# Strassen FFN-out in passes of 8, 8 and 6 units, with all seven products doubled in its all-Strassen output pairs

## The chip, the core and the metric

The kernel runs on one core of a Trainium2 chip. Its time is the device time of one execution in microseconds (us), given as the median of several runs. A profile is the record of one further execution: its span runs from the first to the last instruction, and the execution's own time lies a little above the span. Five engines work side by side, each with its own in-order instruction stream: TensorE (PE, matrix products, with its weight loads listed as PEld), VectorE (DVE), ScalarE (ACT), GpSimd (POOL) and SyncE (SP). SP and POOL also issue the transfers between DRAM and the on-chip memory.

## What is computed

One layer of a decoder on 512 tokens of width 2048, in float32. Cut to what matters here:

```python
h = rmsnorm(x) ; proj = h @ w_in                    # 2048 -> 11264 columns
y_a, y_b = gated spatial mixing, stick-breaking attention
merged = sigmoid(g_a) * (y_a @ w_up_a) + sigmoid(g_b) * (y_b @ w_up_b)
x = x + merged @ w_o
hid = rmsnorm(x) @ w_ffn_in                         # 2048 -> 2 * 5632
x = x + (silu(hid[:5632]) * hid[5632:]) @ w_ffn_out # 5632 -> 2048
x = x + sigmoid(rmsnorm(x) @ w_ple_gate) * (p @ w_ple)
```

The change lies in the last two products, the FFN-out product (5632 to 2048) and the gate product (2048 to 2048), and in how operands for FFN-in and for these two are prepared.

## The kernel before

Activations lie transposed: 128 partitions of features by 512 tokens. A *unit* is a piece of 256 features of the contraction: 2048 features are 8 units (`KU`), the hidden layer's 5632 are 22. An *output pair* is 256 output features. Each operand is held as a high and a low part, and each product is taken as high times high, high times low and low times high (`mm3`, lines 272 to 282: three matrix products).

A unit is multiplied in one of two ways. Plain (P): four weight blocks of 128x128 against 512 tokens, 12 products of 512 columns. Strassen (S): seven products of sums of blocks, each against 256 tokens, 21 products of 256 columns; the seven are put together afterwards by `mix` on DVE and ACT. In a *doubled* Strassen product the high and low halves lie side by side, so high weights take both in one product of 512 columns and low weights one of 256: 14 products per unit for all seven (line 692), each product in a bank of its own, put together by `mix_doubled` (lines 726 to 770) in more and smaller DVE steps. `Pair.__init__` sets `doubled` to 0 as soon as one unit of the pair is plain, so only all-S pairs are doubled. Before the change FFN-in is doubled 7, the input projection 5, FFN-out and gate not at all. A pair with both kinds adds its plain banks at the end in `rest` (line 796).

Weights come by `Weights`: a transfer of raw blocks by SP, for S one more adding transfer by POOL, then splits on ACT (line 343) and DVE (340) and two sums on DVE (359). One such object serves one unit, or two neighbours of the same kind when the first has an even number (`doubles`). Four landing buffers and three slots hold them.

Operands come as `Form`s. A late S form first loads its raw unit (1024 columns of the arena `wholes`, `fetch`), splits it for plain use (`plain_first`, lines 270, 271), and later loads it once more (`fetch_second`) to build the three or four sums (line 509) that Strassen use needs. `PLAIN_UNTIL` says for how many output pairs a unit is used plain: in each FFN-out pass four units become S at pair 1, the others at pair 2. `all_first` (used for the input projection) builds everything from one load. Forms live in the arena `parts`, which holds eight S forms and 1024 columns more. After every one to three products `tick` runs (line 197): it may fetch one of the next three forms (`AHEAD`), build the first of them if its places are free, or else fetch a second load. Loads, weights and stores all go through SP's queue.

FFN-out contracts 22 units in passes of 8, 7 and 7 (`PASSES`). In a pass each of the eight output pairs j takes all units of the pass; passes 2 and 3 load the partial sum of pair j, add to it (`onto`, lines 801 and 805) and store it. In pass 3 the sum is also scaled (line 1225), the residual added (1439), the result x2 stored (1440) and squared for the next norm (957, 961). The next pass's forms join the queue `builds` at the last pair (j = 7), and the gate's eight forms, made of x2[0..7], do so at the last pair of pass 3. The gate is `SSSSSPPP`, with pair 0 all plain; its pair 0 needs all of x2.

Of the kernel before, what the change touches and what calls it, by code (L numbers as in the profile page):

```python
# [19 lines left out]
P = 128  # L20
# [3 lines left out]
KU = D // (2 * P)  # L24
HID = 5632
KH = HID // P
# [3 lines left out]
EPS = 1e-6  # L30

OUT = "SSSSPPPP"
PASSES = 8, 7, 7
PLAIN_UNTIL = 1, 1, 1, 1, 2, 2, 2, 2
GATE = "SSSSSPPP"
PLACE = 7 * 256

AHEAD, WAIT = 3, 2
# [28 lines left out]
def hybrid_layer(  # L67
# [131 lines left out]
    def tick():  # L199

        clock[0] += 1
        last, units = traced()[-1], dict(newest)
        urgent = [f for f in seconds if f.used]
        for f in list(builds)[: 0 if urgent else AHEAD]:
            if not f.there and f.ready() and fits([(wholes, 1024, "old")]):
                f.fetch()
                break
        if builds and builds[0].ready() and builds[0].arrived() and fits(builds[0].sizes):
            builds.popleft().step()
        elif seconds and fits([(wholes, 5 * 256, "old")]):  # L210
# [300 lines left out]
    def twice(x):  # L511
        return x.unsqueeze(1).to_broadcast([P, 2, 256])

    def plain_first(form, raw, gain=None):
# [36 lines left out]
    def all_first(form, raw):  # L551


        b, s, v = cut(raw.f()), take(768, "old"), take(256, "old")
        t, x = cut(s.f()), form.operand()
        split_into(x[:, 0:4, 0], x[:, 0:4, 1], b)
        tt(t[:, 2], b[:, 3], b[:, 2])
        tt(v.f(), b[:, 3], b[:, 1])
        tt(t[:, 0], t[:, 2], b[:, 1])
        tt(t[:, 1], t[:, 0], b[:, 0], ALU.add)  # L560
        give(raw)
        form.at_plain = True
        yield
        yield
        split_into(x[:, 4:7, 0], x[:, 4:7, 1], t)
        give(s)
        yield
        while not form.used:
            yield
        split_into(x[:, 3, 0], x[:, 3, 1], v.f())  # L570
        give(v)

    def late_form(src, ready=always, gain=None, far=False):

# [14 lines left out]
    def strassen_form(src, ready=always, gain=None, raw=PLACE):  # L589

# [216 lines left out]
    def pair(forms, last=False, plain=None, parts_done=None, at=0, home=lambda: None,  # L807
             doubled=0):

        plain = plain or (0,) * len(forms)
        kinds = "".join("P" if n else f.kind for f, n in zip(forms, plain))
        p = Pair(kinds, home, doubled)
        for k, n in doubles(kinds, at):
            slot, ws = next_weights()
            fs = forms[k : k + n]
            p.add(kinds[k], ws, [f.plain() if plain[k] else f.get() for f in fs])
            for f, left in zip(fs, plain[k : k + n]):
                if left == 1:  # L820
                    f.use_plain()
                if last:
                    f.free()
            slots.append(slot)
            if parts_done and k + n == kinds.find("P"):
                last_parts(p, forms[k + n :], parts_done)
                break
        return p

    def plain_left(n, j, until=PLAIN_UNTIL):  # L830

        return tuple(max(0, u - j) for u in until[:n])

    def kinds_of(forms_kinds, j, until=PLAIN_UNTIL):
        return "".join("P" if left else k
                       for k, left in zip(forms_kinds, plain_left(len(forms_kinds), j, until)))

    def last_parts(p, forms, done):

# [435 lines left out]
    def plan_rest():  # L1275
        for j in range(KU):
            for b in "ba":
                plan((w_up_a if b == "a" else w_up_b)[j], "PPPP")
        for j in range(KU):
            plan(w_o[j], OUT)  # L1280
        for j in range(3, KU):
            planned.append((w_ple[j].rearrange("p (b c) -> p b c", b=4), 1, "P"))
        for m in range(KH):
            plan(w_ffn_in[m], ("S" if m else "P") * KU)
        at = 0
        for n in PASSES:
            for j in range(KU):
                plan(w_ffn_out[j], kinds_of("S" * n, j), at)
            at += n
        for j in range(KU):  # L1290
            plan(w_gate[j], GATE if j else "P" * KU)

    def y_form(c, i):
        return plain_form((lambda: y_a[i]) if c == "a" else lambda: load(y_spill[i]),
# [68 lines left out]
             for j in range(KU)}  # L1363
    there = set()

    def spilled_form(kind, n, j, gain=None):
        return (late_form if kind == "S" else plain_form)(
            lambda size=1024: load(spill[n, j], size), lambda: (n, j) in there, gain, far=True)
# [19 lines left out]
    for j in range(5, 8):  # L1388
# [7 lines left out]
    hs = [spilled_form("S", "hid", u) for u in range(KH // 2)]  # L1396
# [9 lines left out]

    for m in range(KH):
        if m == KH - 1:
            builds.extend(hs[: PASSES[0]])
        o = pair(fs, last=m == KH - 1, plain=(0 if m else 1,) * KU, doubled=7).out()  # L1410
# [7 lines left out]
    gs = [spilled_form(k, "x2", j, (g_ple, j)) for j, k in enumerate(GATE)]  # L1418
    norm3 = Norm()
    at = 0  # L1420
    for c, n in enumerate(PASSES):
        units, first = hs[at : at + n], at
        at += n
        for j in range(KU):
            if j == KU - 1:
                builds.extend(hs[at : at + PASSES[c + 1]] if c + 1 < len(PASSES) else gs)
            before = load(spill["sum", j]) if c else None
            x1 = load(spill["x1", j]) if c == len(PASSES) - 1 else None
            pr = pair(units, last=j == KU - 1, plain=plain_left(n, j), at=first)
            if before is None:  # L1430
                nc.sync.dma_start(out=spill["sum", j], in_=pr.out())
                continue
# [14 lines left out]
    for j in range(KU):  # L1447
# [18 lines left out]
            nc.sync.dma_start(out=outT[j][:, a:b], in_=s)  # L1466

        if j == KU - 1:
            pair(gs, parts_done=finish)
# [92 lines left out]
```

## Time and profile before

| | |
|---|---|
| runs before | 2722.21 us median of 3 (2721.26 to 2723.8) |
| profiled execution | 2724.13 us, span 2722.2 us |
| mean granted TensorE clock | 0.994 |
| PE busy | 2668.2 us, 98% of the span |
| DVE busy | 2204.5 us, 81% |
| DMA | 557.74 MB, mean 205 GB/s |

Where the stages begin, by the first product of each in the trace: w_up at 825.1 us, w_o at 1000.8, FFN-in at 1182.1, FFN-out at 2054.9 (pass 2 at 2220.4, pass 3 at 2363.8), gate at 2524.3, end at 2722.2. A view of windows gives for each stretch its length, then busy time and count of instructions for PE, PEld, DVE, ACT and POOL, the granted clock (PEclk, 1.00 is full) and the DMA share with its rate. A view of waits lists what an engine waited for and how long. A busy PE is not a PE at full speed, so the length of a stretch is set against the work in it as well.

### The profile page before, as it was taken

The numbers are of one execution on the slowest core, as the hardware profiler recorded it, in microseconds if no ns is written. First come the engines' busy times: TensorE is split into PE (matmuls) and PEld (weight loads), VectorE is DVE, ScalarE is ACT, GpSimd is POOL, SyncE is SP. The second block draws the span as 40 slices with busy tenths as digits, with TensorE's granted clock in tenths as the row PEclk, the third lists the DMA queues.
The fourth block names the chain that finished last, engine by engine and source line by source line (L and its number), as shares of the span: only waits on it lengthen the run. The fifth ranks groups of instructions, "written<-read, shape, count | busy, mean of one in ns | idle before, by whom it ended". The sixth has DMA issues, their size and how long they took to land.

```text
span 2722.2 us, 44416 instructions
## 1 busy us (share of the span) xinstructions
PE 2668.2 (98%) x16334; PEld 2374.5 (87%) x16334; DVE 2204.5 (81%) x3685; ACT 1405.6 (52%) x2174; POOL 477.3 (18%) x566
## 2 busy tenths in 40 slices
PE   8999999999999999999999999999999999989899
PEld 7888888888998889978888888888888999989698
DVE  8687878788887566679989898989889778789776
ACT  7656565655554343385444444444445444444643
POOL 0232323232210000011111111111111102111110
PEclk9999999999999999999999999999999999999899
DMA  7676777777775466688888888787878879889884
GB/s 227 155 189 167 189 167 190 167 200 180 178 189 193 131 181 200 172 268 209 205 229 201 207 195 215 195 209 195 206 193 263 245 223 283 252 238 277 253 234 124
DMA packets 305883, 557.74 MB, mean 205 GB/s; under 512 B 26752, under 2 KB 155648, under 8 KB 305664
## 3 DMA queue, kind: packets, MB, share of 16 engines
q1 hardware_dynamic: 242496, 447.52, 51.1%
q0 software_dynamic: 63168, 107.37, 24.7%
q8 instruction: 128, 2.10, 0.3%
q14 instruction: 91, 0.75, 0.1%
HBM read 507.61 MB, written 47.19 MB: 204 GB/s over the span
## 4 chain that ended last, share of the span: by engine, by line
PE 86%; DVE 6%; DMA 3%; ACT 2%; issue 2%; POOL 1%; SPq 0%; DVEq 0%; ACTq 0%; POOLq 0%
PE ps L692 40%; PE ps L281 13%; PE ps L282 13%; PE ps L280 13%; PE small L692 4%; DVE wlo L340 2%; DVE parts L271 1%; DVE out L751 1%; DMA wholes<-hid 1%; DMA wholes<-x 1%; PE small L1158 1%; ACT whi L343 1%; PE small L1033 1%; DVE wholes L509 1%; PE small L1108 1%
## 5 line engine op out<-in xcount | busy, mean ns | idle before, releaser
L343 ACT ACTIVATE whi<-wholes 128x1280 fp32r<-128x1280 f32 (+3 forms) x960 | 876.1, 927 | 805.6 <-DVE wholes L359 273.7
L692 PE MATMUL ps<-parts,whi 128*128 128x512 f32 x3384 | 1135.5, 398 | 3.3 <-ACT out L789 2.6
L340 DVE TENSOR_TENSOR wlo<-wholes,whi 128x1280 fp32r<-128x1280 f32 (+3 forms) x960 | 984.3, 1059 | 86.5 <-ACT whi L343 86.0
L281 PE MATMUL ps<-parts,whi 128*128 128x256 f32 (+1 forms) x2799 | 881.2, 315 | 11.1 <-DVE parts L271 10.8
L280 PE MATMUL ps<-parts,whi 128*128 128x256 f32 (+1 forms) x2782 | 869.5, 315 | 21.3 <-ACT parts L270 15.7
L282 PE MATMUL ps<-parts,wlo 128*128 128x256 f32 (+1 forms) x2799 | 878.6, 315 | 0.6 <-DVE wlo L340 0.6
L692 PEld LDWEIGHTS ps<-parts,wlo 128*128 128x128 f32 x3384 | 635.8, 188 | 142.0 <-issue 1.0
L692 PE MATMUL ps<-parts,wlo 128*128 128x256 f32 x3384 | 671.2, 279 | 0.0
L281 PEld LDWEIGHTS ps<-parts,whi 128*128 128x128 f32 x2799 | 536.5, 192 | 51.7 <-DVE parts L271 15.1
L280 PEld LDWEIGHTS ps<-parts,whi 128*128 128x128 f32 x2782 | 531.3, 192 | 57.2 <-ACT parts L270 18.5
L282 PEld LDWEIGHTS ps<-parts,wlo 128*128 128x128 f32 x2799 | 535.6, 192 | 33.1 <-DVE wlo L340 2.5
L692 PEld LDWEIGHTS ps<-parts,whi 128*128 128x128 f32 x3384 | 546.7, 189 | 9.8 <-ACT out L789 3.0
L359 DVE TENSOR_TENSOR wholes<-wholes 128x256 f32<-128x256 f32 (+1 forms) x840 | 348.2, 415 | 24.2 <-issue 3.5
L347 POOL DMA_DIRECT2D wholes<-w_ffn_in x172 | 149.7, 870 | 698.9 <-DVE wholes L359 261.5
L751 DVE TENSOR_TENSOR out<-out,ps 128x256 f32<-128x256 f32 x388 | 160.2, 415 | 125.1 <-ACT out L748 124.6
L347 POOL DMA_DIRECT2D wholes<-w_in x132 | 118.4, 898 | 489.3 <-DMA wholes<-w_in 112.6
L271 DVE TENSOR_TENSOR parts<-wholes,parts 128x1024 fp32r<-128x1024 f32 (+4 forms) x126 | 132.3, 1058 | 25.2 <-ACT parts L270 25.0
L347 POOL DMA_DIRECT2D wholes<-w_ffn_out x79 | 74.1, 939 | 403.3 <-DMA wholes<-w_ffn_out 152.6
L270 ACT ACTIVATE parts<-wholes 128x1024 fp32r<-128x1024 f32 (+4 forms) x126 | 113.7, 920 | 51.0 <-DVE wholes L509 35.9
L692 PE MATMUL small<-parts,whi 128*128 128x512 f32 x344 | 136.2, 397 | 0.0
L718 DVE TENSOR_TENSOR out<-out 128x256 f32<-128x256 f32 x144 | 61.0, 423 | 84.0 <-ACT out L715 81.5
L1400 ACT ACTIVATE out<-out 128x512 f32<-128x512 f32 x44 | 27.9, 633 | 161.1 <-DVE out L1399 161.1
(122 smaller groups left out, 1697.4 us busy)
## 6 DMA issues: line engine op xcount, KB each, us to landing
wholes<-w_ffn_in SPq DMA_DIRECT2D x172, 384.0 KB, 5.6
wholes<-w_in SPq DMA_DIRECT2D x132, 384.0 KB, 5.0
wholes<-w_ffn_in SPq DMA_DIRECT2D x172, 256.0 KB, 4.8
wholes<-w_ffn_in POOLq DMA_DIRECT2D x172, 256.0 KB, 5.4
wholes<-w_in SPq DMA_DIRECT2D x132, 256.0 KB, 4.1
wholes<-w_in POOLq DMA_DIRECT2D x132, 256.0 KB, 4.9
wholes<-w_ffn_out SPq DMA_DIRECT2D x65, 384.0 KB, 5.3
wholes<-x SPq DMA_DIRECT2D x45, 512.0 KB, 5.5
```

What stands on the lines that cost most here:

```text
L270: return (nc.scalar.activation(hi, src, AF.Copy), nc.vector.tensor_tensor(out=lo, in0=src, in1=hi.bitcast(F32), op=ALU.subtract))
L271: nc.vector.tensor_tensor(out=lo, in0=src, in1=hi.bitcast(F32), op=ALU.subtract))
L280: nc.tensor.matmul(ps, sh, mh, start=start, stop=False)
L281: nc.tensor.matmul(ps, sh, ml, start=False, stop=False)
L282: return nc.tensor.matmul(ps, sl, mh, start=False, stop=stop)
L340: in_turn(nc.vector.tensor_tensor(out=self.lo[:, blocks], in0=r, in1=h.bitcast(F32), op=ALU.subtract))
L343: in_turn(nc.scalar.activation(h, r, AF.Copy))
L347: nc.gpsimd.dma_start(out=raw[:, 3:5], in_=self.src[:, 1:3], accum_op=ALU.add)
L359: in_turn(nc.vector.tensor_tensor(out=o, in0=x, in1=y, op=ALU.add))
L692: m = nc.tensor.matmul(out, l, r, start=first and k == 0, stop=last and k == 1)
L718: in_turn(nc.vector.tensor_tensor(out=out, in0=x, in1=y, op=op))
L751: in_turn(nc.vector.tensor_tensor(out=out, in0=x, in1=y, op=op))
```

## The change

- The passes of FFN-out are 8, 8 and 6 units; in the last pass units 4 and 5 are plain throughout, and its first four units turn S at pair 2.
- All-S pairs of FFN-out are doubled in all seven products.
- The gate's forms join `builds` at the start of the last pass. In the gate, units 2, 3 and 4 stay plain in pair 1 as well.
- FFN-in's forms are built by `all_first` from one load; `all_first` itself loses one step of waiting between its two splits, in the input projection too.
- `tick` fetches a form only if places in `parts` for it and for those ahead of it are free along with the raw buffer, or if three raw buffers fit (`fits` adds one more of 1024 columns to what it is asked).
- `plain_left` and `kinds_of` give way to `now`; `pair` is told j and until when each unit is plain.

```diff
-PASSES = 8, 7, 7
-PLAIN_UNTIL = 1, 1, 1, 1, 2, 2, 2, 2
+PASSES = "SSSSSSSS", "SSSSSSSS", "SSSSPP"
+PLAIN_UNTIL = (1, 1, 1, 1, 2, 2, 2, 2), (1, 1, 1, 1, 2, 2, 2, 2), (2, 2, 2, 2, 1, 1)
 GATE = "SSSSSPPP"
+GATE_UNTIL = 1, 1, 2, 2, 2, 1, 1, 1
...
         urgent = [f for f in seconds if f.used]
+        sizes = []
         for f in list(builds)[: 0 if urgent else AHEAD]:
-            if not f.there and f.ready() and fits([(wholes, 1024, "old")]):
+            sizes += [s for s in f.sizes if s[0] is parts]
+            raw = [(wholes, 1024, "old")]
+            if not f.there and f.ready() and (fits(sizes + raw) or fits(raw * 3)):
                 f.fetch()
                 break
...
         give(raw)
         form.at_plain = True
         yield
-        yield
         split_into(x[:, 4:7, 0], x[:, 4:7, 1], t)
...
-    def late_form(src, ready=always, gain=None, far=False):
+    def late_form(src, ready=always, gain=None, far=False, twice=True):
...
-            yield from plain_first(form, w, gain)
+            yield from plain_first(form, w, gain) if twice else all_first(form, w)
             return form.operand()
 
-        return Form("S", steps, [(parts, 2 * PLACE, "place")] + [(wholes, 1024, "low")], ready,
-                    src, far)
+        return Form("S", steps, [(parts, 2 * PLACE, "place")]
+                    + [(wholes, 1024, "low")] * (1 if twice else 2), ready, src, far)
...
-            p.add(kinds[k], ws, [f.plain() if plain[k] else f.get() for f in fs])
-            for f, left in zip(fs, plain[k : k + n]):
-                if left == 1:
+            p.add(kinds[k], ws, [f.plain() if j < until[k] else f.get() for f in fs])
+            for f, m in zip(fs, until[k : k + n]):
+                if j == m - 1:
                     f.use_plain()
...
+    def now(kinds, until, j):
+
+        return "".join("P" if j < n else k for k, n in zip(kinds, until))
...
-    fs = [spilled_form("S", "x1", j, (g_ffn, j)) for j in range(KU)]
+    fs = [spilled_form("S", "x1", j, (g_ffn, j), twice=False) for j in range(KU)]
...
-    for c, n in enumerate(PASSES):
-        units, first = hs[at : at + n], at
-        at += n
+    for c, units in enumerate(hs):
+        first, at = at, at + len(units)
+        if c == len(hs) - 1:
+            builds.extend(gs)
         for j in range(KU):
-            if j == KU - 1:
-                builds.extend(hs[at : at + PASSES[c + 1]] if c + 1 < len(PASSES) else gs)
+            if j == KU - 1 and c < len(hs) - 1:
+                builds.extend(hs[c + 1])
...
-            pr = pair(units, last=j == KU - 1, plain=plain_left(n, j), at=first)
+            pr = pair(units, last=j == KU - 1, j=j, until=PLAIN_UNTIL[c], at=first,
+                      doubled=7)
...
-            o = pair(gs, plain=(0 if j else 1,) * KU).out()
+            o = pair(gs, j=j, until=GATE_UNTIL).out()
```

More of the change, by code (lines that the diff above doesn't have):

```diff
@@ L512, in twice, with plain_first @@
         return x.unsqueeze(1).to_broadcast([P, 2, 256])
-    def plain_first(form, raw, gain=None):
+    def plain_first(form, raw, gain):
         x = form.operand()
@@ L805, in onto, with pair @@
                     nc.vector.tensor_tensor(out=s, in0=s, in1=ps, op=ALU.add)
[L807 to L813, printed above, removed]
+    def pair(forms, last=False, j=0, until=None, parts_done=None, at=0,
+             home=lambda: None, doubled=0):
+        until = until or (0,) * len(forms)
+        kinds = now("".join(f.kind for f in forms), until, j)
         p = Pair(kinds, home, doubled)
@@ L828, in pair @@
         return p
[L830 to L836, printed above, removed]
+    def now(kinds, until, j):
+        return "".join("P" if j < n else k for k, n in zip(kinds, until))
     def last_parts(p, forms, done):
@@ L1285, in plan_rest @@
         at = 0
-        for n in PASSES:
+        for kinds, until in zip(PASSES, PLAIN_UNTIL):
             for j in range(KU):
-                plan(w_ffn_out[j], kinds_of("S" * n, j), at)
-            at += n
+                plan(w_ffn_out[j], now(kinds, until, j), at)
+            at += len(kinds)
         for j in range(KU):
-            plan(w_gate[j], GATE if j else "P" * KU)
+            plan(w_gate[j], now(GATE, GATE_UNTIL, j))
     def y_form(c, i):
@@ L1364, in hybrid_layer, with spilled_form @@
     there = set()
-    def spilled_form(kind, n, j, gain=None):
+    def spilled_form(kind, n, j, gain=None, **how):
         return (late_form if kind == "S" else plain_form)(
-            lambda size=1024: load(spill[n, j], size), lambda: (n, j) in there, gain, far=True)
-    fs = [spilled_form("S", "x1", j, (g_ffn, j)) for j in range(KU)]
+            lambda size=1024: load(spill[n, j], size), lambda: (n, j) in there, gain, far=True,
+            **how)
+    fs = [spilled_form("S", "x1", j, (g_ffn, j), twice=False) for j in range(KU)]
     raw = deque([load(xT[0])])
@@ L1395, in hybrid_layer @@
                   for u in range(KH // 2)})
-    hs = [spilled_form("S", "hid", u) for u in range(KH // 2)]
+    hs = []
+    for kinds in PASSES:
+        hs.append([spilled_form(k, "hid", u)
+                   for u, k in enumerate(kinds, sum(map(len, hs)))])
     def hidden(m, o):
@@ L1408, in hybrid_layer @@
         if m == KH - 1:
-            builds.extend(hs[: PASSES[0]])
-        o = pair(fs, last=m == KH - 1, plain=(0 if m else 1,) * KU, doubled=7).out()
+            builds.extend(hs[0])
+        o = pair(fs, last=m == KH - 1, j=m, until=(1,) * KU, doubled=7).out()
         if m == 0:
@@ L1468, in hybrid_layer @@
         if j == KU - 1:
-            pair(gs, parts_done=finish)
+            pair(gs, j=j, until=GATE_UNTIL, parts_done=finish)
         else:
-            o = pair(gs, plain=(0 if j else 1,) * KU).out()
+            o = pair(gs, j=j, until=GATE_UNTIL).out()
             row3 = norm3.row()
```

1 line of the change is left out of this document (removed).

## The prediction

> **What bounds the kernel now.** I read the page first, then windows by stage, then the waits of PE, then SP and the chain of waits at the two places where PE stands.
>
> ```profile
> PE 2668.2 (98%) x16334; PEld 2374.5 (87%) x16334; DVE 2204.5 (81%) x3685; ACT 1405.6 (52%) x2174; POOL 477.3 (18%) x566
> 985.00:1165.00 180.00, 180.00 (x1118) 162.94 (x1117) 123.40 (x168) 80.76 (x94) 12.18 (x14) 1.00 0.65 191
> 1182.10:1209.70 27.60, 27.60 (x120) 22.63 (x120) 21.51 (x40) 21.86 (x33) 4.79 (x6) 0.94 0.98 302
> 1209.70:1229.20 19.50, 16.90 (x88) 14.44 (x87) 17.23 (x27) 16.29 (x22) 3.27 (x4) 0.91 0.81 233
> 1229.20:2054.90 825.70, 825.26 (x4732) 719.30 (x4731) 734.56 (x1315) 399.13 (x556) 143.54 (x165) 1.00 0.82 205
> 2054.90:2220.40 165.50, 164.26 (x1239) 158.24 (x1238) 131.32 (x209) 79.82 (x96) 22.61 (x26) 1.00 0.84 241
> 2220.40:2363.80 143.40, 143.40 (x1089) 138.50 (x1088) 121.02 (x199) 68.17 (x89) 25.21 (x26) 1.00 0.92 264
> 2363.80:2382.90 19.10, 19.10 (x87) 15.80 (x86) 14.07 (x21) 8.49 (x10) 3.03 (x3) 1.00 0.97 286
> 2382.90:2413.40 30.50, 22.38 (x122) 19.83 (x121) 24.17 (x42) 12.03 (x16) 3.03 (x3) 0.89 0.75 230
> 2413.40:2524.30 110.90, 108.65 (x884) 107.66 (x883) 105.43 (x167) 55.67 (x73) 19.34 (x20) 0.98 0.93 267
> 2524.30:2591.40 67.10, 53.79 (x256) 42.84 (x255) 51.53 (x77) 40.60 (x54) 9.44 (x9) 0.90 0.81 249
> ```
>
> PE bounds nearly everything. Loss sits where a stage begins: FFN-in (1182 to 1229), pairs 1 and 2 of FFN-out's pass 3 (from 2382.9), gate pairs 0 and 1 (from 2524.3). To turn length into loss I need the price of a unit. Stores of finished pairs, four pairs of pass 1 apart and six of FFN-in apart, give it:
>
> ```profile
> 2121.69 0.33 SPq L1431 DMA_DIRECT2D sum<-out  x1
> ...
> 2202.35 0.33 SPq L1431 DMA_DIRECT2D sum<-out  x1
> 1906.30 0.33 SPq L1403 DMA_DIRECT2D hid<-out  x1
> ...
> 2023.45 0.33 SPq L1403 DMA_DIRECT2D hid<-out  x1
> ```
>
> Undoubled S unit: 80.66 / 4 / 8 = 2.521 us. Doubled: 117.15 / 6 / 8 = 2.441. Plain: pass 3's pair 0 has seven in 19.10 us, 2.73.
>
> With these, pass 1 (12 plain, 52 S) is 163.9 us of work in 165.5; pass 2 (10 and 46) 143.3 in 143.4; pass 3, the same units, 143.3 in 160.5, so 17.2 lost. Gate pairs 0 and 1 (11 plain, 5 S) are 42.6 in 67.1, 24.5 lost, the small norm products included. FFN-in (8 plain, 43 doubled pairs) is 861.4 in 872.8, 11.4 lost. What PE waited for in pass 3, in the gate, and what SP waited for at pass 3's start:
>
> ```profile
> PE ps L280 <- ACT parts L270: 6.4, 3, 2.9
> PE ps L281 <- DVE parts L271: 4.0, 2, 3.3
> PE ps L281 <- DVE parts L271: 5.1, 6, 2.3
> PE ps L280 <- ACT parts L270: 4.0, 3, 3.5
> PE ps L280 <- ACT whi L343: 2.5, 3, 1.1
> SPq L500 <- DVE wholes L509: 7.2, 2, 5.5
> SPq L500 <- DVE parts L271: 5.4, 3, 2.3
> 2432.00:2437.00 5.00, 4.68 (x26) 4.69 (x27) 4.15 (x7) 3.35 (x7) 0.88 (x1) 0.66 0.82 219
> ```
>
> The first two lines are pass 3: operand splits were late, 10.4 us in all, while SP's loads (L500) stood until DVE released raw buffers. The last line shows the other 6.8 of the 17.2: after such a gap the granted clock falls for some microseconds.
>
> **The change part by part.** *Units.* Pass 1 becomes 12 plain, 4 undoubled S, 48 doubled: 32.8 + 10.1 + 117.2 = 160.0 us; pass 2 the same; pass 3 (24 plain, 24 undoubled, since a pair with plain units isn't doubled) 65.5 + 60.5 = 126.0. Bare work 446.0 against 450.5 before: only 4.5 us, as 16 more plain units eat half of what doubling saves. The rest must come from the losses.
>
> *Mixing.* The doubled mix costs DVE more:
>
> ```profile
> L751 DVE TENSOR_TENSOR out<-out,ps 128x256 f32<-128x256 f32 x24 | 10.0, 415 | 7.9 <-ACT out L748 7.8
> L751 DVE TENSOR_TENSOR out<-out,p 128x512 f32<-128x512 f32 x4 | 2.8, 691 | 0.1
> L718 DVE TENSOR_TENSOR out<-out 128x256 f32<-128x256 f32 x12 | 5.1, 423 | 11.0 <-ACT out L715 10.7
> L718 DVE TENSOR_TENSOR out<-ps,out 128x512 f32<-128x512 f32 x3 | 2.0, 682 | 0.0
> L340 DVE TENSOR_TENSOR wlo<-wholes,whi 128x1280 fp32r<-128x1280 f32 x17 | 25.2, 1483 | 0.0
> 1800.00:1878.12 78.12, 78.12 (x450) 68.11 (x450) 69.23 (x125) 37.34 (x52) 13.93 (x16) 1.00 0.81 202
> 2293.30:2346.20 52.90, 52.90 (x444) 52.90 (x443) 42.57 (x71) 24.09 (x33) 12.19 (x13) 1.00 0.96 250
> 2441.00:2493.90 52.90, 52.90 (x438) 52.40 (x437) 51.23 (x82) 25.39 (x33) 12.28 (x13) 1.00 0.97 284
> ```
>
> Twelve steps of 256 columns and one of 512 are 5.7 us per pair; the old mix has five and one, 2.8. So 2.9 us more DVE in each of 12 pairs. A pass 2 pair now takes 42.57 / 3 = 14.2; the eighth unit adds half a weight double (1.48 + 0.69 + two steps of 0.42, halved: 1.5), the mix 2.9: 18.6 of a 19.5 us pair. FFN-in's pairs run at 69.23 of 78.12 without loss, but pass 3 from 2413.4 on, at 105.43 of 110.9, lost 5.0 beyond its 105.9 of work. I cost the mix at nothing as such, hidden behind PE; if that cover went, 2.9 x 12 = 35 us would show.
>
> *Losses of the passes.* Pass 1 keeps its 1.7: 161.7, so -3.8. Pass 2 has eight forms like pass 1 but a partial sum in `wholes` and the fuller DVE; between nothing and pass 3's old 17.2, nearest pass 1's row, I take 2.0: 162.0, so +18.6. Pass 3's old stall is second loads too late for pair 1; now no unit is S before pair 2, four need a second load instead of seven, and weights are three objects per pair instead of four. But DVE gets gate forms to build. A pair there is 51.23 / 3 = 17.1 now; it loses one S double (3.0) and a single (1.5), gains a plain double's split (1.2): 13.8 of 15.5; two plain pairs about 9 each; four second halves at about 2.7 and three gate forms at about 4.5 (estimates from the 1.2 and 0.42 steps) make 126 in all, as much as PE's 126.0. I take 4 lost, ends 0 and 12: 130.0, so -30.5. Together -15.7.
>
> *Gate.* The stall is the chain to the last form:
>
> ```profile
> 2533.26 1.22 DVE wholes L801
> ...
> 2537.81 1.22 DVE wholes L1439
> 2539.05 6.73 DMA x<-wholes
> 2545.83 6.51 DMA wholes<-x
> 2552.37 0.73 ACT parts L504
> 2553.13 1.41 DVE parts L619 x2
> ```
>
> PE ended pass 3 at 2524.3; x2[7] was stored at 2539.05 because DVE had other forms to build, came back at 2552.3, usable at 2554.5: 30 us, against seven plain units (19.1) that can run ahead of it, and those had only one free place to be built in early. After the change about three S places are free during pass 3, so units 0 to 2 stand ready, and the last pair ends on two plain units (5.5 us of cover for the mix). I put the store at 9 us after PE's end (five 1024-wide or lesser steps, about 5, and handovers), then 13.2 and 2.1: 24, so about 5 us of gap, 2 to 3 of slow clock, 3 for norm products and remaining splits: 11 lost, between 5 and 24.5. Work grows by 0.6 (three S units plain in pair 1). 43.3 + 11 = 54.3 against 67.1: -12.8.
>
> [...]
>
> *FFN-in's start.* No second loads, and ACT drops two scalings per form; but DVE does four sums per form at once, in the stretch where x1[7] and the norm are made, which PE waits for. Ends: all the 11.4 but the norm products gained (-9), or a like delay again (+8). Between far ends I take -1.5, as ACT (21.86 of 27.6) is the fuller there.
>
> *The rest.* The fetch test is looser than it looks: where places are free it asks what the old one asked. One step of waiting less in `all_first` moves a split by one product group in the first stage. I cost both at nothing, plus or minus 2; w_up's forms find all places free.
>
> Sum: -15.7 - 12.8 - 1.5 = -30.0 on the profiled 2724.13, 2694.1. That execution is 1.9 over the median 2722.21, so 2692.
>
> **The rivals.** *All gaps close.* Passes at bare work (446.0 for 469.4), gate losing 6, FFN-in gaining 5: -23.4 - 17.8 - 5 = -46, 2676. For it: the plan gives every form more time. Against: the x2[7] chain.
>
> *Pass 2 becomes the old pass 3.* Eight second loads, a partial sum in `wholes`, DVE at 95%: it loses 17 instead of 2, 2707; the same again in pass 3 would give 2722. For it stand the SP lines above, against it pass 2's present row, which lost nothing.
>
> *Slower: SP blocks on the gate's early loads.* In pass 3 the load of x2[j] follows its store on SP, and weights queue behind it. The store was 14.8 us after PE's end, 6.7 to land, and new weights took:
>
> ```profile
> wholes<-w_ffn_out SPq DMA_DIRECT2D x65, 384.0 KB, 5.3
> ```
>
> That is 26.8 against 15.5 us of a pair that buffered weights cover: 11.3 for each of five loads made inside pass 3, 56 us, 2748. It decides from 7.1 us per load. Against it: w_o does the same with x1 and its 180.00 us are all PE.
>
> *Short gaps cost no clock.* If the clock stayed full after the remaining gaps, 2 to 3 us less, 2689; the 0.66 window after gaps of at most 3.3 us speaks against it. The Trainium skill ("TensorE: Matmul & The Clock Gate", Part 1) throttles only after at least one idle window of about 3.4 us; by that rule gaps like those would be free, and the trace disagrees with its 0.66.
>
> *The doubling doesn't take.* If mixed kinds kept `doubled` at 0 throughout, 96 units cost 0.08 more: 2700.
>
> **How the numbers follow.** Forecast 0.47 (own range 2684 to 2702), all gaps close 0.18, pass 2 stalls 0.19, short gaps free 0.05, no doubling 0.03, SP blocks 0.08. A measurement tells about 0.2%, 5.4 us, from no change. Slower is the SP case, 0.08; same is the far end of the pass 2 case, 0.04; faster the rest, 0.88. Leaving out SP, that far end and the lowest 0.06 of the closing case: 2672 to 2714.
>
> **What would show it.** Doubled pairs of FFN-out 19.5 us apart; passes near 162, 162 and 130; no PE wait on L270 at pass 3's pair 1; gate pairs 0 and 1 in about 54 us with the x2[7] chain as their last wait. Wrong: waits on L271 in pass 2's pair 1, DVE over 95% with PE gaps in passes 2 or 3, or weights (L343, L340) late in pass 3.

## The result, and the profile after

| | before | after |
|---|---|---|
| median of 4 runs each | 2723.01 us (2721.26 to 2729.43) | 2691.4 us (2687.82 to 2695.73) |
| ratio, 95% interval | 1 | 0.988, 0.9859 to 0.9902 |
| span of the profiled execution | 2722.2 us | 2690.0 us |
| mean granted clock | 0.994 | 0.998 |

The change takes 32 us off, 1.2%. The forecast was 2692. First the engines on the page of after, then its windows by stage (columns as in the windows of before: start and end, length, busy time and count of PE, PEld, DVE, ACT and POOL, granted clock, DMA share, GB/s):

```profile
PE 2653.3 (99%) x15496; PEld 2325.7 (86%) x15496; DVE 2207.7 (82%) x3715; ACT 1388.7 (52%) x2161; POOL 458.2 (17%) x549
```

```profile
1183.60:2049.60 866.00, 864.88 (x4930) 752.88 (x4930) 766.07 (x1368) 428.03 (x597) 152.74 (x174) 1.00 0.82 207
2049.60:2210.20 160.60, 160.59 (x902) 139.50 (x901) 142.61 (x245) 81.09 (x108) 22.68 (x26) 1.00 0.85 246
2210.20:2373.10 162.90, 160.95 (x902) 139.46 (x901) 148.25 (x252) 78.92 (x105) 21.80 (x25) 1.00 0.90 262
2373.10:2407.70 34.60, 33.08 (x145) 26.83 (x144) 27.20 (x41) 13.63 (x16) 2.63 (x3) 1.00 0.80 255
2407.70:2430.40 22.70, 18.64 (x114) 16.55 (x114) 18.20 (x30) 12.39 (x15) 1.75 (x2) 0.92 0.93 298
2430.40:2509.20 78.80, 77.78 (x542) 72.83 (x541) 72.83 (x106) 37.65 (x49) 6.09 (x7) 1.00 0.81 246
2509.20:2555.50 46.30, 45.54 (x228) 38.55 (x227) 37.59 (x55) 29.34 (x41) 5.90 (x7) 1.00 0.89 272
2555.50:2580.30 24.80, 22.80 (x144) 21.01 (x143) 21.05 (x33) 11.83 (x15) 2.85 (x3) 0.93 0.89 275
2580.30:2690.00 109.70, 104.41 (x728) 97.84 (x726) 75.64 (x118) 40.70 (x54) 11.17 (x11) 0.99 0.59 167
```

The rows are FFN-in, pass 1, pass 2, pass 3 in three parts (pairs 0 and 1; pair 2, the first with S units; pairs 3 to 7), then gate pairs 0 and 1, gate pair 2, the rest. Gate pair 2 of before ran from 2591.4 to 2612.2. Against the stages of before:

| | before | after | measured | forecast |
|---|---|---|---|---|
| all before FFN-in | 1182.1 | 1183.6 | +1.5 | 0 |
| FFN-in | 872.8 | 866.0 | -6.8 | -1.5 |
| pass 1 | 165.5 | 160.6 | -4.9 | -3.8 |
| pass 2 | 143.4 | 162.9 | +19.5 | +18.6 |
| pass 3 | 160.5 | 136.1 | -24.4 | -30.5 |
| gate pairs 0 and 1 | 67.1 | 46.3 | -20.8 | -12.8 |
| gate pair 2 | 20.8 | 24.8 | +4.0 | 0 |
| the rest | 110.0 | 109.7 | -0.3 | 0 |
| sum | | | -32.2 | -30.0 |

The start of FFN-in is taken at the first product behind the norm's eight small ones. It lies between 1181.7 and 1185.9 in the kernels of this study, with this change's early edits or without, because the small products fall now earlier and now later among their neighbours: of the 107 products of 512 columns between 1150 us and the first doubled product, 94 come before them in before, 100 in after. So the first two rows belong together: FFN-in ends 5.3 earlier than in before. The sum came out because errors cancel, so its closeness is in part luck: pass 3 fell 6.1 short, and gate pair 2 lost 4.0, while gate pairs 0 and 1 gave 8.0 more than forecast and the first two rows 3.8 more.

What PE waited for in after, first in pass 3, then from the start of the gate to 2600:

```profile
PE ps L284 <- ACT parts L274: 4.6, 3, 2.0
PE ps L286 <- DVE wlo L344: 1.0, 1, 1.0
PE ps L285 <- DVE parts L275: 1.0, 2, 0.6
```

```profile
PE ps L285 <- DVE parts L275: 2.0, 1, 2.0
PE small L944 <- DVE diag L942: 0.8, 1, 0.8
```

Lines 274 and 275 are the splits that stood at 270 and 271. The 10.4 us of split waits in pass 3 are down to 5.6, the gate's many waits to two. The mean clock is 0.004 higher, with fewer gaps left.

### The profile page after: what moved, and what is told of

Same layout as the page of the kernel before. It is cut to its first block, busy times and chain, and to the rows that moved or that the text cites. A ratio compares the mean times of both kernels' runs of the same rounds, so it can differ in the third digit from the quotient of the medians.

```text
span 2690.0 us, 42553 instructions
## 1 busy us (share of the span) xinstructions
PE 2653.3 (99%) x15496; PEld 2325.7 (86%) x15496; DVE 2207.7 (82%) x3715; ACT 1388.7 (52%) x2161; POOL 458.2 (17%) x549
## 4 chain that ended last, share of the span: by engine, by line
PE 85%; DVE 7%; DMA 3%; ACT 2%; issue 2%; POOL 1%; SPq 0%; DVEq 0%; ACTq 0%; POOLq 0%
PE ps L695 47%; PE ps L285 10%; PE ps L286 10%; PE ps L284 10%; PE small L695 6%; DVE wlo L344 2%; DVE out L754 1%; DMA wholes<-x 1%; DVE parts L275 1%; PE small L1157 1%; DMA wholes<-hid 1%; DVE wholes L363 1%; ACT whi L347 1%; DVE wholes L513 1%; PE small L1032 1%
## 5 line engine op out<-in xcount | busy, mean ns | idle before, releaser
L695 PE MATMUL ps<-parts,whi 128*128 128x512 f32 x3960 | 1324.8, 397 | 0.3 <-DVE p L754 0.3
L347 ACT ACTIVATE whi<-wholes 128x512 fp32r<-128x512 f32 (+3 forms) x933 | 866.0, 942 | 787.0 <-DVE wholes L363 274.0
L344 DVE TENSOR_TENSOR wlo<-wholes,whi 128x512 fp32r<-128x512 f32 (+3 forms) x933 | 974.1, 1078 | 85.6 <-ACT whi L347 85.4
L695 PEld LDWEIGHTS ps<-parts,wlo 128*128 128x128 f32 x3960 | 743.7, 188 | 168.1 <-issue 1.0
L695 PE MATMUL ps<-parts,wlo 128*128 128x256 f32 x3960 | 784.3, 279 | 0.1
L285 PE MATMUL ps<-parts,whi 128*128 128x256 f32 (+1 forms) x2070 | 679.5, 329 | 4.8 <-DVE parts L275 4.7
L284 PE MATMUL ps<-parts,whi 128*128 128x256 f32 (+1 forms) x2048 | 668.1, 328 | 12.4 <-ACT parts L274 10.6
L286 PE MATMUL ps<-parts,wlo 128*128 128x256 f32 (+1 forms) x2070 | 677.6, 329 | 1.7 <-DVE wlo L344 1.7
L695 PEld LDWEIGHTS ps<-parts,whi 128*128 128x128 f32 x3960 | 637.8, 189 | 5.9 <-issue 1.0
L285 PEld LDWEIGHTS ps<-parts,whi 128*128 128x128 f32 x2070 | 393.6, 190 | 46.5 <-DVE parts L275 7.3
L284 PEld LDWEIGHTS ps<-parts,whi 128*128 128x128 f32 x2048 | 388.5, 190 | 48.9 <-ACT parts L274 12.7
L286 PEld LDWEIGHTS ps<-parts,wlo 128*128 128x128 f32 x2070 | 393.5, 190 | 36.2 <-DVE wlo L344 3.2
L695 PE MATMUL small<-parts,whi 128*128 128x512 f32 x440 | 174.5, 397 | 0.0
L274 ACT ACTIVATE parts<-wholes 128x1024 fp32r<-128x1024 f32 (+4 forms) x134 | 112.9, 865 | 46.9 <-DVE wholes L513 26.1
L751 ACT ACTIVATE out<-ps 128x256 f32<-128x256 f32 x243 | 91.4, 385 | 47.5 <-PE ps L695 44.0
```

What stands on the lines that cost most here:

```text
L274: return (nc.scalar.activation(hi, src, AF.Copy), nc.vector.tensor_tensor(out=lo, in0=src, in1=hi.bitcast(F32), op=ALU.subtract))
L284: nc.tensor.matmul(ps, sh, mh, start=start, stop=False)
L285: nc.tensor.matmul(ps, sh, ml, start=False, stop=False)
L286: return nc.tensor.matmul(ps, sl, mh, start=False, stop=stop)
L344: in_turn(nc.vector.tensor_tensor(out=self.lo[:, blocks], in0=r, in1=h.bitcast(F32), op=ALU.subtract))
L347: in_turn(nc.scalar.activation(h, r, AF.Copy))
```

## The experiments

Four questions: what the early gate forms do, what closed the gate's gap, what the doubling is worth, and where FFN-in's gain came from. Every time is the median of its runs, with the ratio to the kernel before, run on the same chip, and its 95% interval. Where an edit is to the kernel before, its heading says so.

### Early or late joining of the gate's forms

Two edits to the changed kernel: the gate's forms join the queue of builds at pair 3 of the last pass, or at pair 7 as they did before the change. The diff of the second:

```diff
-        if c == len(hs) - 1:
-            builds.extend(gs)
         for j in range(KU):
+            if c == len(hs) - 1 and j == 7:
+                builds.extend(gs)
```

> The changed kernel, but the gate's forms join the queue at pair 3 of the last pass instead of its start. Pair 2 of the last pass takes 22.7 us for 15.5 of work in the changed kernel, with PE waiting on operand splits. Theory A (the load of x2[0], which waits on SP for its store, and the gate forms' work on DVE delay the last pass's own second loads): pair 2 falls to 15.5 to 18, the span by 4 to 7, to about 2684, as the gate's units 0 to 2 are still ready in time. Theory B (the second loads are late for their own reasons, partial sum and residual filling the raw buffers): pair 2 stays above 20 and the span within 2 of 2690, or grows because the gate's forms come later.

> The changed kernel, but the gate's forms join the queue at the last pair of the last pass, as in the kernel before. If the early forms are what closed the gate's gap: gate pairs 0 and 1 grow from 46.3 to between 56 and 67 (the 67.1 of before), and pair 2 of the last pass falls as in the run with pair 3, so the span is 5 to 15 above 2690. Rival: the gap closed because the last pass is shorter and leaves places free; then gate pairs 0 and 1 stay under 50 and the span falls by 3 to 7.

Joining at pair 3: 2690.7 us (2689.21 to 2693.38), ratio 0.9878 (0.9863 to 0.9893). Joining at pair 7: 2684.92 us (2681.55 to 2691.7), ratio 0.9864 (0.9843 to 0.9884). So that a few us can be told, the late joining and the changed kernel unaltered ran once more, side by side:

> The run with the gate's forms joining at pair 7, once more beside the changed kernel. Theory: the early joining costs 6 to 7 us through pass 3, so this is at 2683 to 2687 and the changed kernel at 2689 to 2693. Rival: the first difference was scatter; then the two agree within 3 us.

> The changed kernel itself, unaltered, for a comparison on the same chip: 2689 to 2693 by the theory that its early joining costs it 6 to 7 us, within 3 us of the late-joining run by the rival.

Late: 2686.19 us (2683.51 to 2688.25), ratio 0.9859 (0.9844 to 0.9874). The changed kernel: 2692.08 us (2690.13 to 2694.42), ratio 0.9882 (0.9867 to 0.9896). The ranges do not overlap: the late joining is 5.9 us faster than the changed kernel, and 1.4% faster than the kernel before; it has the lowest ratio of this study, though the changed kernel with the old fetch test, further below, comes within the scatter (0.986). Both times came out as the theory of these two expectations had them. The windows of the late joining in that second run: pass 3 in the same three parts, gate pairs 0 and 1, gate pair 2:

```profile
2371.50:2405.30 33.80, 33.04 (x145) 26.81 (x144) 27.17 (x41) 13.59 (x16) 2.63 (x3) 1.00 0.82 263
2405.30:2422.30 17.00, 16.15 (x111) 14.77 (x110) 15.28 (x26) 8.26 (x10) 1.75 (x2) 1.00 0.95 295
2422.30:2500.10 77.80, 77.80 (x546) 73.12 (x545) 71.21 (x103) 35.98 (x45) 6.09 (x7) 1.00 0.85 257
2500.10:2550.50 50.40, 47.42 (x229) 37.97 (x228) 43.61 (x63) 37.27 (x49) 6.82 (x7) 1.00 0.89 277
2550.50:2572.10 21.60, 21.02 (x143) 19.43 (x142) 20.14 (x32) 10.37 (x14) 2.36 (x3) 1.00 0.94 294
```

Read beside after's rows: pass 3's pair 2 takes 17.0 for 22.7, ACT's 12.39 falls to 8.26 and DVE's count from 30 to 26. In after the gate's first form is scaled and split in that pair, ahead of the second loads that turn pass 3's own units into S; with the late joining it is not. In the second run of the changed kernel the pair took 20.8 and the whole pass 134.6, so against that run the late joining gives the pass 6.0, which is the difference of the medians. In the gate the late joining costs 4.1 in pairs 0 and 1 and gives 3.2 back in pair 2; the two together take 72.0, against 71.1 in after. The changed kernel's second run, gate pairs 0 and 1 and then pair 2, has 73.2:

```profile
2505.50:2553.00 47.50, 45.94 (x228) 38.47 (x227) 37.83 (x55) 29.30 (x40) 6.07 (x7) 1.00 0.88 266
2553.00:2578.70 25.70, 22.90 (x144) 21.04 (x144) 20.95 (x33) 11.82 (x15) 2.68 (x3) 0.93 0.84 261
```

So the early forms bring the gate nothing that can be told, close to the rival of the run at pair 7, and pass 3 pays for them. With the joining at pair 3, pair 2 of the pass is relieved too, as theory A said, but the median did not fall: the bill comes later. Pair 2 and the whole of pass 3:

```profile
2408.30:2426.10 17.80, 16.31 (x110) 14.80 (x109) 15.17 (x26) 8.25 (x10) 1.67 (x2) 1.00 0.92 286
2374.20:2509.80 135.60, 130.24 (x799) 116.52 (x798) 119.41 (x177) 64.77 (x82) 10.47 (x12) 0.99 0.85 264
```

The whole pass is at 135.6, as with the changed kernel's 136.1: pair 2 gave 4.9 and later pairs took it back, pairs 5 and 6 above all, whose S products take 11.8 and 14.2 us where the other pairs have 10.1. The loss moved; it did not go.

### The gate's old S start, and S at pair 1 in pass 3

Two further edits on top of the late joining. The first makes the gate's five S units S from pair 1, as before the change; the second makes pass 3's four S units S at pair 1 instead of 2.

```diff
-GATE_UNTIL = 1, 1, 2, 2, 2, 1, 1, 1
+GATE_UNTIL = 1, 1, 1, 1, 1, 1, 1, 1
```

```diff
-PLAIN_UNTIL = (...), (...), (2, 2, 2, 2, 1, 1)
+PLAIN_UNTIL = (...), (...), (1, 1, 1, 1, 1, 1)
```

> The run with the gate's forms joining at pair 7 (2685 us, gate pairs 0 and 1 in 50.5 us), with the gate's units 2, 3 and 4 turning S at pair 1 again. Theory (the second pair of plain use gives the second loads time): gate pairs 0 and 1 take 8 to 16 us more, about 2696. Rival (the shorter last pass alone closed the gap): within 3 us of 2685.

> The same run with the gate's forms joining at pair 7, but the last pass's four S units turn S at pair 1 instead of pair 2. Theory (the old stall came from second loads too late for pair 1): pair 1 of the last pass stands again for 6 to 13 us, less 0.8 of cheaper units, about 2694. Rival (the smaller pass and fewer second loads removed it): pass 3 stays within 3 us of its 129.3, about 2685.

The old gate: 2701.69 us (2700.7 to 2702.45), ratio 0.9908 (0.9893 to 0.9923). S at pair 1: 2702.53 us (2695.53 to 2705.47), ratio 0.9908 (0.989 to 0.9925). The stage that each edit touches, gate pairs 0 and 1 of the first with its largest wait, then pass 3 of the second:

```profile
2503.10:2569.50 66.40, 51.37 (x255) 41.66 (x255) 49.13 (x74) 39.67 (x52) 8.89 (x9) 0.90 0.79 238
```

```profile
PE ps L284 <- ACT parts L274: 9.6, 2, 7.3
```

```profile
2371.10:2515.00 143.90, 133.00 (x837) 120.44 (x835) 120.35 (x172) 60.84 (x74) 10.41 (x12) 0.95 0.80 242
```

With only the old gate list back, pairs 0 and 1 take 66.4 for 50.4, nearly the 67.1 of before, although the last pass leaves the same places in `parts` and still ends on plain units. Three units that stay plain for one pair longer are worth 16 us here, while their arithmetic in that pair is 0.6 dearer. In pass 3 the same device is worth 15.3 (143.9 for 128.6), more than the 6 to 13 expected. A pair 1 with fewer S units needs fewer second loads at once, and the long waits lie at the splits (L274) of such forms. On top of the other changes this device carries most of both gains; what it is worth without them is the next question.

### The same device alone, in the kernel before

An edit to the kernel before: the last pass turns S at pair 2 throughout, and gate units 2 to 4 stay plain in pair 1. Passes of 8, 7, 7 and all the rest stay.

```diff
-PLAIN_UNTIL = 1, 1, 1, 1, 2, 2, 2, 2
+PLAIN_UNTIL = (1, 1, 1, 1, 2, 2, 2, 2), (1, 1, 1, 1, 2, 2, 2), (2,) * 7
+GATE_UNTIL = 1, 1, 2, 2, 2, 0, 0, 0
```

> The kernel before (passes of 8, 7 and 7, no doubling in FFN-out, two loads in FFN-in, old fetch test), with one thing added: the last pass's seven units and the gate's units 2, 3 and 4 stay plain for one more pair. Theory from the two runs that took this away (14.6 us in pass 3, 15.9 in the gate): that alone is most of the gain; pass 3 goes from 160.5 to between 147 and 153, gate pairs 0 and 1 from 67.1 to between 50 and 56, the median from 2725 to about 2700. Rival (it works only with the shorter last pass and its free places): above 2712.

2709.92 us (2708.07 to 2711.64), ratio 0.9947 (0.9932 to 0.9961), a gain of 0.5%: between the 2700 of the theory and the 2712 of the rival, so neither holds as it stands. Pass 3, and gate pairs 0 and 1:

```profile
2367.60:2521.10 153.50, 148.59 (x1053) 140.45 (x1052) 137.69 (x215) 73.42 (x93) 23.18 (x24) 0.98 0.90 268
2521.10:2576.40 55.30, 48.68 (x230) 39.11 (x229) 47.93 (x72) 37.61 (x51) 6.83 (x7) 0.97 0.85 267
```

Pass 3 gains 7.0 on its 160.5, the gate 11.8 on its 67.1: about two fifths of what the whole change brings, and with no doubling and no new cut of the passes. It stays short of the 15 and 16 above, so the device is worth more with the rest of the change than without it. In pass 3 seven second loads now fall due together at pair 2, and PE waits there for a split (line 271 is what 270 was):

```profile
PE ps L281 <- ACT parts L271: 3.5, 1, 3.5
```

### The doubling

Three edits. The doubling taken out of the changed kernel's FFN-out:

```diff
             pr = pair(units, last=j == KU - 1, j=j, until=PLAIN_UNTIL[c], at=first,
-                      doubled=7)
+                      )
```

> The changed kernel without doubling in FFN-out (twelve all-S pairs with 21 products per unit again). Theory: only the price of a unit changes, 2.52 for 2.44 us in 96 units, 7.7 in all: passes 1 and 2 at about 164.5 and 166.7 for 160.6 and 162.9, span about 2698. Rival: the larger mix on DVE costs part of it back through waits at pass ends, so that without doubling the span rises by less than 4.

2696.57 us (2694.8 to 2697.82), ratio 0.9898 (0.9883 to 0.9913). Passes 1 and 2 without it:

```profile
2048.90:2213.00 164.10, 164.09 (x1238) 158.23 (x1237) 131.21 (x208) 80.12 (x96) 22.62 (x26) 1.00 0.85 242
2213.00:2377.60 164.60, 164.31 (x1239) 158.04 (x1238) 134.42 (x210) 77.22 (x93) 21.73 (x25) 1.00 0.88 259
```

By these rows the doubling is worth 3.5 in pass 1 and 1.7 in pass 2, of 32. But pass 2 of the changed kernel took 162.9 in after and 161.1 in its second run, with the same products; the difference lies ahead of its all-S pairs. In these, stores of neighbouring pairs are 20.16 us apart without doubling (from 2154.64 to 2174.80) and 19.53 with it (in after, from 2155.40 to 2174.93): 0.63 in each of 12 pairs, 7.6 in all, as the theory had it. Of that 4.5 to 5.2 show in the medians, between theory and rival. In pass 1 the mix is hidden behind PE as forecast: DVE does 142.61 for 131.21, 11.4 more, and PE does not stand. Next, an edit to the kernel before, doubling alone with the passes as they were:

```diff
-            pr = pair(units, last=j == KU - 1, plain=plain_left(n, j), at=first)
+            pr = pair(units, last=j == KU - 1, plain=plain_left(n, j), at=first, doubled=7)
```

> The kernel before, with only the doubling in FFN-out's all-S pairs added (passes of 8, 7 and 7 units as before). Theory by the unit prices: 132 units in 18 pairs at 0.08 us less, 10.6 us in all, so about 2712 against 2723, if the larger mix stays hidden. Rival: pass 3, whose DVE was busy 105.4 of 110.9 us, has no room for 2.9 us more per pair; it then takes 5 to 15 us longer and the kernel is no faster than 2720.

2730.24 us (2727.38 to 2734.44), ratio 1.0016 (1.0007 to 1.0026): slightly slower, as the rival said. Passes 1 and 2, and pairs 2 to 7 of pass 3:

```profile
2056.10:2217.00 160.90, 160.74 (x903) 139.43 (x902) 142.82 (x245) 81.06 (x108) 22.64 (x26) 1.00 0.86 247
2217.00:2358.10 141.10, 141.02 (x794) 122.11 (x793) 134.28 (x242) 68.75 (x101) 24.01 (x25) 1.00 0.92 264
2409.00:2531.50 122.50, 110.71 (x589) 89.92 (x587) 118.40 (x205) 59.14 (x89) 20.20 (x21) 0.98 0.87 250
```

Passes 1 and 2 gain 4.6 and 2.3, and pass 3 gives back 11.6 (122.5 for the 110.9 quoted in the prediction). There DVE is busy for 118.40 of 122.50: the cover of the mix is gone and DVE is the bound. Pass 2 of this run still gains with DVE busy for 134.28 of 141.10. Last, on top of the late joining, a last pass of six S units, all doubled, with no unit that stays plain:

```diff
-PASSES = "SSSSSSSS", "SSSSSSSS", "SSSSPP"
-PLAIN_UNTIL = (...), (...), (2, 2, 2, 2, 1, 1)
+PASSES = "SSSSSSSS", "SSSSSSSS", "SSSSSS"
+PLAIN_UNTIL = (...), (...), (2, 2, 2, 2, 2, 2)
```

> The late-joining run, but all six units of the last pass are Strassen from pair 2 on, so that its all-S pairs are doubled too. By TensorE alone a pair falls from 15.5 to 14.7 us and the kernel by 5. Theory (DVE bounds such a pass: about 17 to 18 us per pair by the sum of its steps, as in the old pass 3 with doubling, where pairs took 19.4 for 17.1): pairs 2 to 7 take 17 to 18 us and the span is 8 to 15 above 2680.

2724.86 us (2720.82 to 2731.54), ratio 0.9998 (0.9988 to 1.0008): the whole gain is gone, where the theory had 8 to 15 us of loss. Its pairs 2 to 7, then gate pairs 0 and 1:

```profile
2406.80:2526.60 119.80, 101.80 (x505) 82.82 (x503) 109.80 (x183) 51.36 (x74) 12.39 (x15) 0.90 0.78 226
2526.60:2592.90 66.30, 52.71 (x228) 41.45 (x229) 50.53 (x78) 37.07 (x48) 6.84 (x7) 0.90 0.78 240
```

These six pairs hold 36 doubled units, 88 us of work at 2.441, and take 119.8, with DVE busy for 109.80 and the clock down to 0.90. PE's longest waits there are for DVE: 6.2 us in all on the mix, 4.1 on weights and 3.4 on operand splits. The changed kernel's mixed pairs 2 to 7 hold more work on PE (93 us by the prediction's prices) and take 101.5. The two plain units of the last pass cost PE 0.9 us per pair (15.5 for 36 x 2.441 / 6 = 14.6) and spare DVE second forms, weight sums and, since a pair with a plain unit is not doubled, the larger mix. The second row is as weighty: against the late joining, the six pairs lose 25.0 and the gate 15.9. Gate pairs 0 and 1 take 66.3 us again, with a wait of 6.9 on one operand split, although units 2 to 4 stay plain in pair 1. So that device does not close the gate's gap behind every kind of last pass. Whether the doubled mix or the missing plain units are to blame was not tried apart.

### FFN-in's start

Two edits to the changed kernel, each taking one of the two parts back: the second loads of FFN-in's forms, and the old fetch test.

```diff
-    fs = [spilled_form("S", "x1", j, (g_ffn, j), twice=False) for j in range(KU)]
+    fs = [spilled_form("S", "x1", j, (g_ffn, j)) for j in range(KU)]
```

```diff
-            if not f.there and f.ready() and (fits(sizes + raw) or fits(raw * 3)):
+            if not f.there and f.ready() and fits(raw):
```

> The changed kernel, but FFN-in's forms are built with a second load again (plain_first). Theory: the second scalings on ACT and the second loads caused the loss after FFN-in's pair 0; the wait of the first doubled products comes back and FFN-in grows from 865.8 by 5 to 7 us, span about 2696. Rival: the loss went because of the new fetch test or other ordering; then the span stays within 2 of 2690.

> The changed kernel with the old fetch test (a form is fetched as soon as its raw buffer fits). If the test does nothing, as the prediction had it: within 3 us of 2691. Rival: early raw loads of forms without a place fill the buffers and hold back second loads, so that FFN-in's start, or the last pass with the gate's forms in the queue, loses 5 us and more.

With second loads: 2702.71 us (2696.28 to 2703.23), ratio 0.9916 (0.9898 to 0.9933). With the old test: 2688.8 us (2683.76 to 2692.95), ratio 0.986 (0.9844 to 0.9876), not to be told from the changed kernel, as expected. The first one's FFN-in and pair 0 of pass 1, and its largest wait in that pair; then FFN-in of the second:

```profile
1182.00:2049.90 867.90, 865.28 (x4928) 752.74 (x4928) 769.82 (x1378) 434.76 (x608) 151.62 (x174) 1.00 0.83 210
2049.90:2077.70 27.80, 23.92 (x97) 19.02 (x96) 25.11 (x41) 13.51 (x17) 1.72 (x2) 0.94 0.76 241
```

```profile
PE ps L285 <- DVE parts L275: 3.9, 2, 3.5
```

```profile
1183.90:2051.60 867.70, 867.68 (x4936) 755.23 (x4937) 773.77 (x1384) 433.80 (x607) 151.60 (x174) 1.00 0.82 207
```

FFN-in takes 872.8 with neither part, 867.9 with the new test alone, 867.7 with one load alone, 866.0 with both. By its end, which the shifting start does not touch, it comes 5.0, 3.3 and 5.3 earlier than in before (2054.9). So either part alone brings most of it, and the two do not add up. Neither theory nor rival of the second loads holds: FFN-in grew by 2, not by 5 to 7, and the median rose by 11. They cost more after FFN-in than in it: pair 0 of pass 1, whose work is 21.8, takes 27.8, PE standing 3.5 us on one operand split, and the clock at 0.94. Why these forms of pass 1 come late then was not tried. The profiled execution was also the fastest of the four, at 2696.28; the others took 2702.21 to 2703.23, and no trace shows where they lost the 6 to 7 us more.

## Why the prediction was right

**Units and doubling.** The price of a doubled unit held: the six all-S pairs of pass 1 take 117.5 us in after, 2.45 a unit, and passes 1 and 2 came within 1.1 us of their terms. The 7.7 us that doubling 96 units was to save are there in the spacing of the all-S pairs (7.6). The "2.0" lost in pass 2 measured 2.9 in after and 1.1 in the second run of the same kernel, so it holds within the scatter.

**The mix behind PE.** "I cost the mix at nothing as such, hidden behind PE": right for passes 1 and 2, and for pass 3 only because the change undoubles it there. The doubling of the old pass 3, and of a last pass of six S units, shows the 35 us warned of, in part. The price itself was too high: the 2.9 us per pair, a sum of single steps, measured 1.9 in pass 1 and 2.2 in pass 3 of the old kernel (118.40 for 105.43 in six pairs). Steps listed with 0.42 us start 0.34 apart in the trace, so they overlap. That the mixed pairs of pass 3 spare DVE was counted in the forecast (13.8 of 15.5 in a pair), and it is what lets the change gain there.

**Pass 3.** "I take 4 lost, ends 0 and 12" measured 10.1 (136.1 against 126.0), and 8.6 in the second run. The term was too small and its mechanism half right: second loads came late, but DVE was not full, busy for 18.20 of the 22.7 us of pair 2. Late joining, with 2.6 lost, shows what the other 6.0 to 7.5 are: gate forms built in the pass, which the forecast had counted as DVE work that just fits. The count held for the sum of the pass (DVE did 118.2 us; the items listed add up to 125, written as 126), but not for the pair in which the second loads are due.

**The gate.** Here the number was nearer than its reasoning. "Units 0 to 2 stand ready", from three free S places, was to shrink the gap from 24.5 to 11 lost. With late joining those units are not built ahead, and pairs 0 and 1 still take 50.4, better than the 54.3 forecast; with the old gate list they take 66.4 though the places are free. The step that failed is "The stall is the chain to the last form". With the device alone in the kernel before, x2[7] is stored 14.7 us after pass 3's end, as late as the 14.8 of before, and yet 11.8 of the 24.5 lost are gone. With late joining it is stored after 10.9 us, with the old gate list on top after 11.6, and pairs 0 and 1 take 50.4 and 66.4. So the second loads for five S units in pair 1 were about half of the old gap, and on top of the late joining 16 of the 23.8 lost (66.4 for 42.6 of work). The chain is still there. SP in after, at the store and the reload of x2[7]:

```profile
2521.03 0.33 SPq L1445 DMA_DIRECT2D x<-wholes  x1
2521.41 0.42 SPq L504 DMA_DIRECT2D wholes<-x  x1
...
2524.69 0.80 SPq L504 DMA_DIRECT2D wholes<-x  x2
```

The store is issued 11.8 us after pass 3's end at 2509.2, where I had put 9. But it is covered: from 2522.8 on PE takes products of pair 1's two S units, which are ready, ahead of the last plain units of pair 0. What I did not see at all is gate pair 2, for which the three units that stayed plain take their second loads: 4.0 lost in after, 0.8 with late joining.

**FFN-in.** The -1.5 was a choice between -9 and +8 and measured -6.8, or -5.3 with the row above it. The four sums per form, done at once in the stretch before FFN-in, brought no delay that shows.

**The rivals.** All gaps closing would have left 2676; 10.1 lost in pass 3 and 7 in the gate speak against it. Pass 2 did not become the old pass 3: 2.9 lost for 17, with one wait of 1.3 us on an operand split in its pair 0. SP did block on the early loads, for less than the 7.1 us a load that was to decide. SP's waits at the start of pass 3 in after:

```profile
SPq L504 <- DMA x<-wholes: 4.1, 2, 3.5
SPq L504 <- DVE wholes L513: 3.5, 3, 2.7
```

The load of x2[j] stood for its own store, 4.1 us in two; in the whole pass it is 13.4 us in six, none above 3.5. The late joining takes these loads out of the pass along with DVE's splits, so how its 6.0 to 7.5 us divide between SP and DVE is not told apart.

**The signs.** Doubled pairs 19.5 us apart, and passes 1 and 2 near 162, came true. Pass 3 (136.1 for 130), the gate's 54 us with the chain as its last wait (46.3, with no wait on it in the list), and the absence of a split wait at pass 3's pair 1 (one of 1.5 us stayed) did not.

**The clock after a gap.** The rival by which short gaps are free fell once more. In after PE stood several times in pair 2 of pass 3, and behind that the clock fell to half for 3.4 us:

```profile
2420.00:2425.00 5.00, 2.99 (x20) 2.33 (x19) 3.41 (x5) 1.06 (x1) 0.00 (x0) 1.00 0.87 222
2425.00:2430.00 5.00, 5.00 (x23) 4.46 (x23) 4.17 (x8) 4.54 (x7) 0.00 (x0) 0.66 0.92 325
2425.30:2428.70 3.40, 3.40 (x15) 3.11 (x14) 2.91 (x5) 3.10 (x5) 0.00 (x0) 0.50 0.90 336
```

The longest of these waits was 2.2 us from 2417.2, counted from start to start of two products less the length of one; it ended 5.7 us before the fall, and the others were shorter. In the second run of the same kernel the same waits came, the longest 1.92 us from 2414.5, and the clock stayed full:

```profile
2417.00:2422.00 5.00, 2.99 (x20) 2.33 (x20) 3.34 (x5) 1.06 (x1) 0.00 (x0) 1.00 0.93 239
2422.00:2427.00 5.00, 5.00 (x34) 4.55 (x33) 4.24 (x8) 4.91 (x7) 0.00 (x0) 1.00 0.81 296
```

It would be wrong to read from this an edge at 2 us. With the old gate list on top of the late joining a wait of 2.50 us from 2535.0 cost no clock (first row), and with FFN-in's second loads back one of 1.48 us from 2446.5, with a shorter one ahead of it, had the clock at half right behind it (second row):

```profile
2537.70:2542.70 5.00, 4.97 (x41) 4.98 (x42) 4.66 (x7) 3.28 (x3) 0.00 (x0) 1.00 0.75 208
2448.50:2451.90 3.40, 3.40 (x18) 3.40 (x17) 3.33 (x8) 0.38 (x1) 0.00 (x0) 0.50 1.00 323
```

So the length of one wait does not decide; what does, these runs leave open. The Trainium skill ("TensorE: Matmul & The Clock Gate", Part 1) lets the clock fall after an idle window of about 3.4 us; the gaps ahead of these falls are shorter, and the trace disagrees.

## What to carry to other kernels

When an operand has a cheap first form and a dear second one, let the switch come in portions: a unit that stays in the cheap form for one pair longer cost 0.2 us of PE here and saved 4 to 5 of standing in the changed kernel, 2 to 4 in the kernel before. It did not do so everywhere: behind the last pass of six doubled S units the gate takes as long as ever, with its three units plain for that pair. Building ahead is no gain by itself: work that joins the queue early takes its turns in front of work that is due, so count what the queue holds in the pair where something is due, not over the whole stage. And before moving work from the bound engine to a helper, look at the helper's share in each stage: the same doubling gave 4.6 us where DVE came to 0.89 of the time, 2.3 where it came to 0.95, and took 11.6 where it came to 0.97.

## What was not expected of the hardware

Weight loads are listed as busy for 158.24 of the 165.5 us of pass 1 in before, and doubling takes a quarter of the products and their loads away (1239 to 902), yet the pass gets only 3% shorter. The columns that pass through PE are the same, 21 x 256 or 7 x (512 + 256) per unit, and the time follows these much more closely than the number of instructions or the listed share of the loads.

The clock answers almost equal waits differently. 3.4 us at half speed are 1.7 us of work, most of what parts the 22.7 us of pair 2 in after from the 20.8 in the second run of the same kernel.

Still open are how the two parts of FFN-in's gain overlap, and what is left of the gate's loss with late joining (7.1 us in pairs 0 and 1, in which the list of waits has no single one over 0.7 us).
